# Two MLPs of a diffusion backbone: TensorE keeps the program's order instead of a planner's

## The chip, the cores and the metric

The kernel runs on one core of a Trainium2 chip. The time is device microseconds of one execution, and the median of the runs counts. TensorE (PE) multiplies matrices, VectorE (DVE) and ScalarE (ACT) work on vectors, GpSimd (POOL) does some of the vector work too, and SyncE (SP) issues the transfers. Each engine takes its own instructions strictly in the order in which they were written to its queue, and engines wait for one another by semaphores.

## The reference, cut to what matters

512 latent tokens and 256 context tokens, 1024 wide, pass two layers. Each layer is an attention sub-layer and then an MLP. Context tokens go through the MLP of layer 0 only, so that MLP has 768 tokens (6 tiles of 128) and the one of layer 1 has 512 (4 tiles).

```python
def sq_relu_mlp(h, w1, w2):          # w1: 1024 x 4096, w2: 4096 x 1024
    return jnp.square(jax.nn.relu(h @ w1)) @ w2

x = layer_norm(alpha * x + g_m * sq_relu_mlp(x * (1.0 + sc_m) + sh_m, mlp_w1[i], mlp_w2[i]),
               ln_g[i, 1], ln_b[i, 1])
```

The scales, shifts and gates (`sc_m`, `sh_m`, `g_m` and the like) come from a modulation map: a vector of 1024 numbers times `w_ada`, a 1024 x 6144 matrix per layer.

## The kernel before, in words

Every float32 operand is split into a high and a low part (`split_hi` on ACT, line 62; `split_lo` on DVE, line 65), and a product becomes three: high x high, high x low, low x high. For weights the parts are the tiles `wh` and `wl`, for hidden units `hh` and `hl`. A weight tile is loaded into one of 3 buffers `raw`, then split into one of 6 pairs of buffers `wh`/`wl`.

`mlp` (line 940) cuts the 4096 hidden units into 32 blocks of 128, taken as 16 groups of `G = 2`. For group c there are two kinds of work on PE:

- `up_mm(c)`, lines 977, 980 and 981: the first-matrix products, hidden = w1 x tokens, into the PSUM tag `big` (2 buffers). Layer 0: 96 products of 384 columns; layer 1: 48 of 512. `up_end(c)` then makes the hidden parts: relu on ACT (988), square on DVE (989), `hh` on ACT, `hl` on DVE. There are 4 buffers of each, two groups' worth.
- `down(i, hid, w2)`, lines 89 to 91 through `mm3`: the second-matrix products of token tile i, 12 products of 512 columns into two buffers of the PSUM tag `one` (4 buffers in all, so two tiles' worth). DVE adds each half to the accumulator `yacc` (line 1059; in group 0 ACT copies it, 1057).

In the program, layer 0 writes out group 0's first-matrix products ahead of the loop, layer 1 those of groups 0 and 1. The loop runs over c = 0 to 13: weights `w2(c)`, first-matrix products of c + 1 where they are not done, then `down` of group c for all tiles. At c = 13 each tile also gets `yacc * gate` (1061) and `+ alpha * x` (1062), where x is reloaded (`xr`, 2 buffers) and scaled by POOL (328, 329). The tail takes groups 14 and 15 together: four blocks, 24 products per token tile, then residual, LayerNorm and, in layer 1, the output.

In layer 0 the loop also carries the modulation vectors of later sub-layers as a filler: 56 steps, 5 per group, each loading a 512 KB slice of `w_ada` into `raw` and adding it, scaled, to `xr` accumulators (ACT 206, DVE 197, POOL 208). After 8 steps an `end` runs on PE: products with `onehot` (215), then, after a DVE addition (`modrow`, 132), for four of the seven vectors two transposes (152). `Fill` calls `end` after `lag` further calls; one call follows each token tile.

What sets the order: the order of each engine's queue is chosen at build time by a planner that simulates the program. Of the instructions that its simulation finds ready it takes the one that stands first in the program. So first- and second-matrix products of different groups may be mixed on PE. `tc.manual_schedule(engines=...)` takes an engine out of the planner's hands: its instructions keep program order. The planner also hands out the buffers of a tag.

Of the kernel before, what the change touches and what calls it, by code (L numbers as in the profile page):

```python
# [12 lines left out]
F32R = mybir.dt.float32r  # L13
# [6 lines left out]
P = 128  # L20
# [14 lines left out]
G = 2  # L35
R = 2
# [3 lines left out]
def backbone(ctx, tc, a, out):  # L40
# [3 lines left out]
    nc = tc.nc  # L44

    def pool(stack, name, bufs=1, side="left", space=None):
        kw = {"space": space} if space is not None else {"side": side}
        return stack.enter_context(tc.tile_pool(name=name, bufs=bufs, reuse_waits="tile", **kw))
# [6 lines left out]
    def big():  # L55
        return ps.tile([P, 2, 512], F32, name="big", tag="big", bufs=2)

    def one():
        return ps.tile([P, 512], F32, name="one", tag="one", bufs=4)

    def split_hi(dst, src):
        return nc.scalar.copy(out=dst, in_=src)  # L62
# [323 lines left out]
    accs = {t: pair[t // 2 - 1][:, t % 2, :] if t >= NCT else one() for t in range(NT)}  # L386
# [127 lines left out]
    fill = Fill(steps, 6)  # L514
# [425 lines left out]
    def mlp(layer, tiles, aH, aL, x_src, late, zst, lnst, fill, before_tail, finish):  # L940

        nt = len(tiles)
        ntok = nt * P
        n = NH // G
        st = ExitStack()
        hp = pool(st, "hp")
        ups = {}

        def up(c):
            if c not in ups:
                ws = [weight(a["mlp_w1"][layer, c * G + j]) for j in range(G)]
                if nt == 6:
                    Hs = [big()[:, :, 0:384] for j in range(G)]
                    parts = [[(H[:, i, :], i * 384, i * 384 + 384) for i in range(2)] for H in Hs]
                else:
                    H = big()
                    Hs = [H[:, j : j + 1, :] for j in range(G)]
                    parts = [[(h[:, 0, i * 256 : i * 256 + 256], i * 256, i * 256 + 256) for i in range(2)] for h in Hs]  # L960
                    if c > 1:
                        parts = [[(h[:, 0, :], 0, 512)] for h in Hs]
                ups[c] = (ws, Hs, parts)
            return ups[c]

        def up_mm(c, which=None, js=range(G), hooks={}):
            ws, Hs, parts = up(c)
            for j in js:
                wh, wl = ws[j]
                for i, (o, s, e) in enumerate(parts[j]):  # L970
                    if which is not None and i != which:
                        continue
                    for k in range(KD):
                        ks = slice(k * P, (k + 1) * P)
                        for f in hooks.get(k, []):
                            f()
                        mm = nc.tensor.matmul(o, wh[:, ks], aH[:, k, s:e], start=(k == 0), stop=False)  # L977
                        if k in hooks:
                            tc.keep_in_program_order(mm)
                        nc.tensor.matmul(o, wh[:, ks], aL[:, k, s:e], start=False, stop=False)  # L980
                        nc.tensor.matmul(o, wl[:, ks], aH[:, k, s:e], start=False, stop=(k == KD - 1))  # L981

        def up_end(c):
            out_h = []
            for Hv in up(c)[1]:
                r = hp.tile([P, ntok], F32, name="r", tag="r", bufs=2)
                rv = r.rearrange("p (c w) -> p c w", c=Hv.shape[1])
                nc.scalar.activation(rv, Hv, AF.Relu)
                nc.vector.tensor_tensor(out=r, in0=r, in1=r, op=ALU.mult)
                hh = hp.tile([P, ntok], F32R, name="hh", tag="hh", bufs=G * R)  # L990
                hl = hp.tile([P, ntok], F32R, name="hl", tag="hl", bufs=G * R)
                split_hi(hh, r)
                split_lo(hl, r, hh)
                out_h.append((hh, hl))
            return out_h

        def w2_of(c, gate=None):
            return [weight(a["mlp_w2"][layer, c * G + j], gate=gate) for j in range(G)]

        def down(i, hid, w2):  # L1000
            accs = [one(), one()]
            cols = slice(i * P, (i + 1) * P)
            m = len(hid)
            for hf in range(2):
                cs = slice(hf * 512, hf * 512 + 512)
                for j in range(m):
                    mm3(
                        accs[hf], hid[j][0][:, cols], hid[j][1][:, cols], w2[j][0][:, cs], w2[j][1][:, cs],
                        j == 0, j == m - 1,
                    )  # L1010
            return accs

        def temp():
            return hp.tile([P, ntok], F32, name="r", tag="r", bufs=2)[:, 0:512]

        first = range(1 if nt == 6 else 2)
        for c in first:
            up_mm(c, 0, range(G if c < first[-1] else G - 1))
        after, n_late = [], len(late)

        def act_step():
            after[:] = late.pop(0)()

        hooks = {}
        for k in range(n_late):
            hooks.setdefault(((5, 5, 7, 7) if layer == 0 else (2, 2, 7, 7))[k], []).append(act_step)
        up_mm(first[-1], 0, [G - 1], hooks)
        for c in first:
            up_mm(c, 1)
        hid = {c: up_end(c) for c in first}  # L1030
        zst.close()
        yp = pool(st, "yp")
        yacc = [yp.tile([P, D], F32, name=f"yacc{t}") for t in range(nt)]
        ln = LN(lnst, layer, 1, 2, 2)
        ln.gain(2 * layer)
        fill = Fill(fill(ln), 0)
        nfill = -(-len(fill.steps) // (n - R - 1))
        for c in range(n - R):
            with ExitStack() as order:
                for ins in after if c == 0 else []:  # L1040
                    order.enter_context(tc.issue_after(ins))
                w2 = w2_of(c)
                if c + 1 not in hid:
                    up(c + 1)
            if c + 1 not in hid:
                up_mm(c + 1)
                hid[c + 1] = up_end(c + 1)
            for i, t in enumerate(tiles):
                if c == n - R - 1:
                    x = ln.x_tile(x_src(t))  # L1050
                    g = ln.gate_tile(stream(t))
                    ln.affine(x, x)
                accs = down(i, hid[c], w2)
                for hf in range(2):
                    cs = slice(hf * 512, hf * 512 + 512)
                    if c == 0:
                        nc.scalar.copy(out=yacc[i][:, cs], in_=accs[hf])
                    else:
                        nc.vector.tensor_tensor(out=yacc[i][:, cs], in0=yacc[i][:, cs], in1=accs[hf], op=ALU.add)  # L1059
                if c == n - R - 1:  # L1060
                    nc.vector.tensor_tensor(out=yacc[i], in0=yacc[i], in1=g, op=ALU.mult)
                    nc.vector.scalar_tensor_tensor(
                        out=yacc[i], in0=x, scalar=ALPHA, in1=yacc[i], op0=ALU.mult, op1=ALU.add
                    )
                fill(i < nfill)

        one_gate = ln.gate_tile(stream(tiles[0])) if stream(tiles[0]) == stream(tiles[-1]) else None
        w2, hs = [], hid[n - R]
        for c in range(n - R + 1, n):
            w2 += w2_of(c - 1, one_gate)  # L1070
            up_mm(c)
            hs = hs + up_end(c)
        w2 += w2_of(n - 1, one_gate)
        fill.rest()
        ln.close_x()
        before_tail(ln, temp, yacc)
        for i, t in enumerate(tiles):
            accs = down(i, hs, w2)
            z = yacc[i]
            g = ln.gate_tile(stream(t))  # L1080
            for hf in range(2):
                cs = slice(hf * 512, hf * 512 + 512)
                if one_gate is not None:
                    nc.vector.tensor_tensor(out=z[:, cs], in0=z[:, cs], in1=accs[hf], op=ALU.add)
                    continue
                tmp = temp()
                nc.vector.tensor_tensor(out=tmp, in0=accs[hf], in1=g[:, cs], op=ALU.mult)
                eng = nc.gpsimd if i < nt - 1 else nc.vector
                eng.tensor_tensor(out=z[:, cs], in0=z[:, cs], in1=tmp, op=ALU.add)
            finish(ln, t, i, z)  # L1090
        st.close()
# [413 lines left out]
```

## Time and profile before

| | |
|---|---|
| median of 3 runs | 1697.6 us (1696.79 to 1701.78) |
| the profiled execution | 1703.23 us |
| its span | 1701.4 us |
| granted TensorE clock, mean | 0.989 |
| PE busy | 1629.9 us (96%) |
| DVE busy | 1111.5 us (65%) |
| ACT, POOL busy | 719.5 us (42%), 450.6 us (26%) |
| first product of the layer 0 MLP | at 412.5 us |
| first product of the layer 1 MLP | at 1316.9 us |

The span runs from the first to the last instruction; the execution's own time is 1.8 us longer. All stretches are in microseconds from the span's start. A timeline row gives start, duration, engine, line, operation, output <- inputs, shapes and count; a bracket tells how long the engine sat idle before it and which instruction ended the wait. Products are pipelined: a row's duration is longer than the distance to the next start, and what a product costs in a dense stretch is that distance.

### The profile page before, as it was taken

Reading aid. Unit: us, or ns where it says so; the run is one execution under the profiler, and the core shown is the slowest. Engines: PE = TensorE matmul, PEld = TensorE weight load, DVE = VectorE, ACT = ScalarE, POOL = GpSimd, SP = SyncE. Lnnn points to the kernel's source line nnn. Section 1 sums busy time; section 2 is a strip of 40 time slices with the busy share of each in tenths; the row PEclk is TensorE's granted clock in tenths of the full one; section 3 lists DMA queues with packets and bytes.
Section 4 is the critical chain, followed back from the end, with each engine's and each line's share of the span. In section 5 each row is a group of like instructions: output and inputs, shape, how many; then the busy total and the mean of one; then the engine's idle time right before and its main releaser. Section 6 shows DMA issues by size and latency. Waiting matters only on the chain.

```text
span 1701.4 us, 23714 instructions
## 1 busy us (share of the span) xinstructions
PE 1629.9 (96%) x9266; PEld 1369.1 (80%) x9266; DVE 1111.5 (65%) x1700; ACT 719.5 (42%) x1317; POOL 450.6 (26%) x317
## 2 busy tenths in 40 slices
PE   8997998999999999999999899999999999999996
PEld 6775776778888888898889798888778888888884
DVE  4778778755756666556447776766658655555577
ACT  3324666644633344333122356666663532222221
POOL 0247889000323345224003431000004200000034
PEclk9998999999999999999999999999999999999998
DMA  8312113033434356344212232001013533322322
GB/s 323 133 66 90 51 57 100 26 136 112 161 122 138 112 184 198 114 147 146 68 50 85 73 104 90 1 1 38 21 60 122 182 99 99 99 98 88 99 75 75
DMA packets 51969, 172.05 MB, mean 101 GB/s; under 512 B 6776, under 2 KB 6928, under 8 KB 51856
## 3 DMA queue, kind: packets, MB, share of 16 engines
q1 hardware_dynamic: 51824, 170.51, 29.8%
q8 instruction: 73, 1.20, 0.3%
q14 instruction: 40, 0.33, 0.1%
q10 hardware_dynamic: 32, 0.02, 0.0%
HBM read 161.03 MB, written 9.47 MB: 100 GB/s over the span
## 4 chain that ended last, share of the span: by engine, by line
PE 68%; DVE 12%; DMA 7%; POOL 6%; ACT 4%; issue 2%; SPq 0%; DVEq 0%; POOLq 0%; ACTq 0%
PE one L89 9%; PE one L91 9%; PE one L90 9%; PE big L977 7%; PE big L981 6%; PE big L980 6%; DMA araw<-in_w_ada_dram 4%; PE one L731 4%; PE one L917 2%; PE one L921 2%; PE one L918 2%; DVE wl L65 2%; PE one L707 2%; POOL aacc L208 2%; DMA raw<-in_mlp_w_dram 2%
## 5 line engine op out<-in xcount | busy, mean ns | idle before, releaser
L62 ACT CAST wh<-raw 128x1024 fp32r<-128x1024 f32 (+3 forms) x172 | 171.9, 1016 | 399.3 <-PE one L91 213.2
L65 DVE TENSOR_TENSOR wl<-raw,wh 128x1024 fp32r<-128x1024 f32 (+3 forms) x172 | 219.8, 1291 | 173.1 <-ACT wh L62 171.6
L977 PE MATMUL big<-actH,wh 128*128 128x384 f32 (+2 forms) x800 | 280.4, 351 | 1.6 <-ACT wh L62 1.6
L981 PE MATMUL big<-actH,wl 128*128 128x384 f32 (+2 forms) x800 | 279.7, 350 | 0.8 <-DVE wl L65 0.8
L980 PE MATMUL big<-actL,wh 128*128 128x384 f32 (+2 forms) x800 | 279.6, 350 | 0.0
L89 PE MATMUL one<-wh,hh 128*128 128x512 f32 x640 | 256.3, 402 | 12.6 <-ACT hh L62 7.0
L91 PE MATMUL one<-wh,hl 128*128 128x512 f32 x640 | 254.5, 399 | 5.3 <-DVE hl L65 5.3
L90 PE MATMUL one<-wl,hh 128*128 128x512 f32 x640 | 255.5, 399 | 1.3 <-DVE wl L65 1.3
L1059 DVE TENSOR_TENSOR yacc<-yacc,one 128x512 f32<-128x512 f32 x260 | 174.0, 682 | 109.9 <-PE one L91 109.6
L208 POOL TENSOR_TENSOR xr<-xr,raw 128x1024 f32<-128x1024 f32 x49 | 129.7, 2647 | 244.8 <-ACT raw L206 229.6
L977 PEld LDWEIGHTS big<-actH,wh 128*128 128x128 f32 x800 | 150.1, 188 | 15.0 <-ACT wh L62 2.4
L981 PEld LDWEIGHTS big<-actH,wl 128*128 128x128 f32 x800 | 150.1, 188 | 14.1 <-DVE wl L65 1.4
L980 PEld LDWEIGHTS big<-actL,wh 128*128 128x128 f32 x800 | 150.2, 188 | 12.3 <-issue 0.4
L89 PEld LDWEIGHTS one<-wh,hh 128*128 128x128 f32 x640 | 122.0, 191 | 44.5 <-ACT hh L62 8.0
L691 ACT ACTIVATE prob<-big,nm 128x768 f32<-128x768 f32 x128 | 116.2, 908 | 92.2 <-DVE nm L690 91.8
L91 PEld LDWEIGHTS one<-wh,hl 128*128 128x128 f32 x640 | 121.5, 190 | 35.0 <-DVE hl L65 6.2
L90 PEld LDWEIGHTS one<-wl,hh 128*128 128x128 f32 x640 | 122.1, 191 | 27.5 <-DVE wl L65 1.7
L328 POOL TENSOR_TENSOR xr<-xr,ln_g 128x1024 f32<-128x1024 f32 x14 | 37.2, 2658 | 390.9 <-DMA xr<-xres 384.6
L690 DVE TENSOR_REDUCE nm<-big 128x1 f32<-128x768 f32 x128 | 119.8, 954 | 31.8 <-PE big L1360 19.0
L707 PE MATMUL one<-ident,prob 128*128 128x128 f32 x832 | 104.8, 275 | 2.9 <-ACT pT L710 2.0
L731 PE MATMUL one<-pT,V 128*64 128x256 f32 x768 | 98.0, 391 | 5.7 <-DVE pT L712 4.5
L707 PEld LDWEIGHTS one<-ident,prob 128*128 128x128 f32 x832 | 96.0, 142 | 6.8 <-ACT pT L710 2.7
(245 smaller groups left out, 2822.9 us busy)
## 6 DMA issues: line engine op xcount, KB each, us to landing
raw<-in_mlp_w_dram SPq DMA_DIRECT2D x128, 512.0 KB
raw<-in_w_ada_dram SPq DMA_DIRECT2D x56, 512.0 KB
sraw<-in_w_ada_dram SPq DMA_DIRECT2D x16, 512.0 KB
araw<-in_w_ada_dram SPq DMA_DIRECT2D x32, 256.0 KB
raw<-in_w_o_dram SPq DMA_DIRECT2D x16, 512.0 KB
xr<-xres SPq DMA_DIRECT2D x14, 512.0 KB
raw<-in_w_qkv_dram SPq DMA_DIRECT2D x12, 512.0 KB
xres<-z SPq DMA_DIRECT2D x10, 512.0 KB
```

The costliest lines, as they stand in the source:

```text
L62: return nc.scalar.copy(out=dst, in_=src)
L65: return nc.vector.tensor_tensor(out=dst, in0=src, in1=hi.bitcast(F32), op=ALU.subtract)
L89: nc.tensor.matmul(o, lh, rh, start=start, stop=False)
L90: nc.tensor.matmul(o, lh, rl, start=False, stop=False)
L91: nc.tensor.matmul(o, ll, rh, start=False, stop=stop)
L208: nc.gpsimd.tensor_tensor(out=accs[s], in0=accs[s], in1=dst, op=ALU.add)
L707: nc.tensor.transpose(tp[:, j * P : (j + 1) * P], pts[j % 2][:, k * P : (k + 1) * P], ident)
L731: nc.tensor.matmul(acc[64 * hh : 64 * hh + 64, 0:256], v(kts[n], hh), PT[:, :, n, hh, :], start=(n == 0), stop=(n == len(kts) - 1),)
L977: mm = nc.tensor.matmul(o, wh[:, ks], aH[:, k, s:e], start=(k == 0), stop=False)
L980: nc.tensor.matmul(o, wh[:, ks], aL[:, k, s:e], start=False, stop=False)
L981: nc.tensor.matmul(o, wl[:, ks], aH[:, k, s:e], start=False, stop=(k == KD - 1))
L1059: nc.vector.tensor_tensor(out=yacc[i][:, cs], in0=yacc[i][:, cs], in1=accs[hf], op=ALU.add)
```

## The change

PE's queue in the loop and in the first part of the tail of both MLPs is pinned to program order. In layer 1 the program is moved so that first-matrix products run two groups ahead (`ahead = 2`) with three groups' worth of `hh`/`hl` buffers; layer 0 stays one ahead. `Fill`'s lag goes from 0 to 2. In the tail, the first two token tiles are begun with three of the four blocks, both of them, before the fourth block follows for both; after that the pin ends.

```diff
+        ahead = 1 if nt == 6 else 2
...
-                hh = hp.tile([P, ntok], F32R, name="hh", tag="hh", bufs=G * R)
-                hl = hp.tile([P, ntok], F32R, name="hl", tag="hl", bufs=G * R)
+                hh = hp.tile([P, ntok], F32R, name="hh", tag="hh", bufs=G * (ahead + 1))
+                hl = hp.tile([P, ntok], F32R, name="hl", tag="hl", bufs=G * (ahead + 1))
...
-        def down(i, hid, w2):
-            accs = [one(), one()]
+        def down(i, hid, w2, accs=None, js=None):
+            accs = accs or [one(), one()]
...
-                for j in range(m):
+                for j in range(m) if js is None else js:
...
-        fill = Fill(fill(ln), 0)
+        fill = Fill(fill(ln), 2)
         nfill = -(-len(fill.steps) // (n - R - 1))
+
+        pinned = ExitStack()
+        pinned.enter_context(tc.manual_schedule(engines={nc.tensor.engine}))
         for c in range(n - R):
             with ExitStack() as order:
                 for ins in after if c == 0 else []:
                     order.enter_context(tc.issue_after(ins))
                 w2 = w2_of(c)
-                if c + 1 not in hid:
-                    up(c + 1)
-            if c + 1 not in hid:
-                up_mm(c + 1)
-                hid[c + 1] = up_end(c + 1)
+                for d in range(c + 1, c + ahead + 1):
+                    if d not in hid:
+                        up(d)
+            for d in range(c + 1, c + ahead + 1):
+                if d not in hid:
+                    up_mm(d)
+                    hid[d] = up_end(d)
...
         for c in range(n - R + 1, n):
             w2 += w2_of(c - 1, one_gate)
-            up_mm(c)
-            hs = hs + up_end(c)
+            if c not in hid:
+                up_mm(c)
+                hid[c] = up_end(c)
+            hs = hs + hid[c]
         w2 += w2_of(n - 1, one_gate)
         fill.rest()
         ln.close_x()
         before_tail(ln, temp, yacc)
+        m = len(hs)
+        begun = {i: down(i, hs, w2, None, range(m - 1)) for i in range(2)}
+        for i in range(2):
+            down(i, hs, w2, begun[i], [m - 1])
+        pinned.close()
         for i, t in enumerate(tiles):
-            accs = down(i, hs, w2)
+            accs = begun[i] if i in begun else down(i, hs, w2)
```

## Rows read from the trace of the kernel before

**Rows 1.** Stretches: length, busy PE, PEld, DVE, ACT, POOL (instructions), granted clock, DMA.
```profile
449.00:640.00 191.00, 182.37 (x927) 159.45 (x926) 120.44 (x123) 78.93 (x86) 64.16 (x24) 1.00 0.44 143
640.00:905.00 265.00, 264.83 (x1341) 237.00 (x1340) 148.28 (x170) 84.12 (x88) 67.38 (x27) 1.00 0.36 121
905.00:960.00 55.00, 50.18 (x228) 43.01 (x228) 45.85 (x39) 10.10 (x12) 25.34 (x10) 0.94 0.25 82
1343.00:1352.00 9.00, 6.22 (x19) 4.72 (x20) 8.92 (x8) 4.56 (x7) 4.15 (x2) 0.81 0.30 104
1352.00:1660.00 308.00, 308.00 (x1324) 248.35 (x1324) 176.12 (x218) 89.39 (x116) 18.62 (x7) 1.00 0.29 94
1660.00:1690.00 30.00, 25.90 (x100) 20.09 (x98) 23.74 (x33) 4.54 (x7) 11.98 (x8) 0.89 0.13 45
```

**Rows 2.** Timeline of ACT and PE in layer 1's steady state.
```profile
1517.08 2.00 ACT L62 CAST wh<-raw 128x1024 fp32r<-128x1024 f32 x2 [8.26 <-PE one L91]
1520.81 1.05 ACT L62 CAST wh<-raw 128x1024 fp32r<-128x1024 f32 x1 [1.73 <-PE big L980]
1526.41 1.05 ACT L62 CAST wh<-raw 128x1024 fp32r<-128x1024 f32 x1 [4.55 <-PE big L980]
...
1526.21 0.40 PE L981 MATMUL big<-actH,wl 128*128 128x512 f32 x1
1526.44 0.39 PE L89 MATMUL one<-wh,hh 128*128 128x512 f32 x1
```

**Rows 3.** Timeline of PE where layer 1's first second-matrix products begin.
```profile
1342.93 0.50 PE L89 MATMUL one<-wh,hh 128*128 128x512 f32 x1 [1.09 <-ACT hh L62]
...
1347.83 0.79 PE L91 MATMUL one<-wh,hl 128*128 128x512 f32 x1 [2.78 <-DVE hl L65]
...
1350.98 0.52 PE L89 MATMUL one<-wh,hh 128*128 128x512 f32 x1
```

**Rows 4.** Timeline of DVE, POOL and PE at layer 1's tail.
```profile
1649.32 1.21 DVE L1061 TENSOR_TENSOR yacc<-yacc,gate 128x1024 f32<-128x1024 f32 x1
1661.99 3.27 POOL L329 TENSOR_TENSOR xr<-xr,ln_b 128x1024 f32<-128x1024 f32 x1
1662.91 3.42 DVE L1061 TENSOR_TENSOR yacc<-yacc,gate 128x1024 f32<-128x1024 f32 x1
...
1669.92 0.79 PE L89 MATMUL one<-wh,hh 128*128 128x512 f32 x1 [3.61 <-ACT hh L62]
...
1675.20 0.54 PE L89 MATMUL one<-wh,hh 128*128 128x512 f32 x1
```

**Rows 5.** Timeline of PE at layer 0's tail.
```profile
943.19 0.50 PE L89 MATMUL one<-wh,hh 128*128 128x512 f32 x1 [2.25 <-ACT hh L62]
...
946.50 0.79 PE L91 MATMUL one<-wh,hl 128*128 128x512 f32 x1 [2.57 <-DVE hl L65]
...
952.07 0.39 PE L89 MATMUL one<-wh,hh 128*128 128x512 f32 x1
```

**Rows 6.** Timeline in layer 0's loop: a wait for a PSUM buffer, two filler ends.
```profile
530.48 0.50 PE L89 MATMUL one<-wh,hh 128*128 128x512 f32 x1 [2.81 <-DVE yacc L1059]
...
564.70 1.09 PE L215 MATMUL one<-xr,onehot 128*32 128x256 f32 x16
565.72 0.50 PE L89 MATMUL one<-wh,hh 128*128 128x512 f32 x1
565.92 0.42 DVE L132 TENSOR_TENSOR modrow<-one,brow 128x256 f32<-128x256 f32 x1 [0.42 <-PE one L215]
570.03 0.38 PE L152 MATMUL one<-ident,modrow 128*128 128x128 f32 x2
...
601.52 2.40 POOL L208 TENSOR_TENSOR xr<-xr,raw 128x1024 f32<-128x1024 f32 x1 [2.46 <-ACT raw L206]
611.97 0.50 PE L89 MATMUL one<-wh,hh 128*128 128x512 f32 x1
614.07 0.41 DVE L132 TENSOR_TENSOR modrow<-one,brow 128x256 f32<-128x256 f32 x1
```

## The prediction, made before the changed kernel was run

> **What bounds the kernel now.** I read the page's shares first: PE is busy nearly all of the span, so the question is where inside the two MLPs it is not. The table of stretches answers that [rows 1]. In layer 1 from 1352 to 1660 us PE is busy 308.00 of 308.00 us with 1324 recorded products, 0.233 us each, at the full clock; in layer 0 from 640 to 905 us it is busy 264.83 of 265.00. No order can be faster there. What can be won lies at four places: the first part of layer 0's loop (191.00 - 182.37 = 8.6 us idle), layer 0's tail, and layer 1's beginning and tail, where the granted clock also falls below 1 (0.94, 0.81, 0.89).
>
> Next comes the timeline at those places. At layer 1's beginning PE waits 1.09 us for `hh` and 2.78 us for `hl` of the hidden groups that were finished last; then 7 starts take 3.15 us (1347.83 to 1350.98), 1.5 us more than at 0.233 [rows 3]. At layer 1's tail it waits 3.61 us for `hh`, and 12 starts take 5.28 us, 2.5 too many [rows 4]. At layer 0's tail it waits 2.25 and 2.57 us, and 13 starts take 5.57 us, 2.5 too many [rows 5]. The slow starts are 0.43 us apart, the lower of the clock's two levels (1.2 instead of 2.4 GHz), right behind a wait of about 3 us. So these three places hold 5.4, 6.1 and 7.3 us. In layer 0's loop a typical wait is for DVE to empty a PSUM buffer, the longest one 2.81 us [rows 6]. All four together: 27.4 us, 1.6% of the time. That is the ceiling.
>
> **The change part by part.** The sum is made against the profiled execution, 1703.2 us (span 1701.4); the median of the runs, 1697.6, lies 5.6 below it, and I carry the difference over to it.
>
> *Steady state.* No product is added or removed. In layer 1 the planner already runs two groups ahead: at 1526.44 second-matrix products start 0.23 us after the last first-matrix product, too soon to use what that one made, so they use an earlier group [rows 2]. The pin writes down nearly the same order, only unmixed. What it could break is the supply of weights. Six pairs of buffers hold three groups' halves; a new split waits for a used one. The trace shows pairs of splits released by the end of second-matrix work (line 91, 1517.08) and pairs released by first-matrix work (line 980, 1520.81 and 1526.41), always as soon as a pair is free [rows 2]. So a freed buffer goes to the next weight in the program. In the new order the first-matrix products of group c + 2 finish before `down` of c starts, their buffers take the first-matrix weights of c + 3, and those are split 11.2 us (48 x 0.233) before they are needed. Cost 0; DVE has 176.12 of 308 us of work there [rows 1]. The transfers of w1 move one group forward on SP, in the order in which the planner had them already.
>
> *Layer 1's beginning.* The first-matrix products of group 2, 48 x 0.233 = 11.2 us, now stand before `down` of group 0. The hidden parts that PE waits for end at 1347.8 [rows 3], and PE would ask for them about 1353 instead of 1341.7. The waits go, and with them the low clock. What is late next is `wl` of group 2's first block, which the third of these products needs; its buffer comes free while group 1's products still run. Between 0 and -5.4; I take -5.4.
>
> *Layer 1's tail.* Group 15's first-matrix products move in front of `down` of group 13, so its hidden parts have 48 more products' time, 11.2 us, plus the first six of the tail. The wait was 3.61 us. It goes, the low clock too: -6.1. Against it: at group 13 DVE has per tile two additions, line 1061 and line 1062, and in the old order PE's 11.2 us of group 15 came behind that work and gave DVE time. Bound on the other side: two of the contended steps of 3.42 us [rows 4] delay the emptying of PSUM by 6.8, of which the spare pair of PSUM buffers hides one token tile (12 x 0.233 = 2.8): +4. I take -6.1, because the emptying reads PSUM and comes first in the program.
>
> The Trainium skill (SBUF — State Buffer, Who interferes with whom) speaks against this: a DVE step with two SBUF inputs and a GpSimd step that reads SBUF exclude each other for a whole instruction. The trace agrees: line 1061 takes 1.21 us alone and 3.42 us beside POOL's line 329 [rows 4]. By that rule every such step of the tail that meets POOL would take the long time, and the tail would win nothing; that is the first rival.
>
> *Layer 0's tail.* Here the order stays one ahead, so group 15 is still made last. New is that tiles 0 and 1 do three blocks each before the fourth: its block is needed 36 products, 8.4 us, into the tail instead of 9 products. The third block is still needed after 6 products, 1.4 us, as before, and DVE is as backed up as before (45.85 busy of 55 us, [rows 1]). Between 0 and -7.3; I take the middle, -3.6.
>
> *The filler in layer 0's loop.* Four of the seven ends have transposes. On PE the planner had put other products between line 215 and line 152: 565.72 to 570.03 [rows 6]. Pinned, the transposes stand right behind line 215 and wait for DVE's `modrow`; behind them on PE wait the next token tile's 12 products, behind these DVE's additions, which have nothing else to do for it. Price from two rows: 565.92 + 0.42 - 565.72 = 0.6 us where DVE was free, 614.07 + 0.41 - 611.97 = 2.5 us where it was not [rows 6]. I take 1.5: 4 x 1.5 = +6 (bounds +2.4 and +10). The lag of 2 instead of 0 puts an end one call, one token tile, later. That is cover for its accumulators: the tightest was done at 603.9 and read at 610.9 [rows 6], 7 us earlier. The two accumulators come free 2.8 us later, the next vector's transfers and steps (SP, ACT, DVE, POOL) with them; POOL is busy 64.16 of 191 us there [rows 1] and takes that up.
>
> *Emptying PSUM in layer 0's loop.* The old order mixed first-matrix products between token tiles, the new one runs six tiles in one stretch, 72 x 0.233 = 16.8 us. DVE must empty 12 halves in it, and its filler steps stand in between. Fewer pauses for DVE within a stretch, but none of this work in the 16.9 us of the first-matrix stretch. Between -8.6 (all waits go) and +22 (second rival); nearest is the row itself, so I take 0.
>
> Sum: -5.4 - 6.1 - 3.6 + 6 + 0 = -9.1. Profiled execution 1694.1, median **1688.5**, told as 1688.
>
> **The rivals.** *Backlog (no change).* DVE and POOL share out the last groups' work as they do now, and both tails win nothing: -5.4 + 6 = +0.6, so 1698. For it: DVE is busy 23.74 of 30 and 45.85 of 55 us at the tails [rows 1]. Against it: in layer 1 the hidden parts are now due 11 us later than made.
>
> *Emptying falls behind (slower).* Place: `down` of groups 1 to 11 in layer 0, while the filler runs. PE's order no longer holds first-matrix products that are ready while DVE is late, so every late emptying stops PE. Price: one wait of 2.81 us [rows 6] in each of 11 groups is 31 us in place of 8.6: +22.3. With the sum above +13.2, so 1711. It decides from the point where DVE's work inside one stretch exceeds 16.8 us plus the spare token tile's 2.8. For it: DVE is at 120.44 of 191 us [rows 1], and half of its work could fall into the stretch beside the 12 additions. Against it: DVE's filler steps go by when slices land, which is spread evenly.
>
> *Buffers by a fixed rotation (slower).* If weights took the six buffers in turn, first-matrix weights of the next group would wait for `down` before them in every group: a split of 1.05 and a low part of 1.2 us, less two products, 1.8 us x 26 groups = 47, so 1736. The alternating releases speak against it [rows 2].
>
> *All waits go (faster still).* -27.4 with the low transposes' price, +2.4: -25, so 1673; half of the loop's and layer 0's tail's waits gives 1679. For it: PE's queue then never depends on a simulated time that the chip doesn't keep. Against it: DVE and POOL slow each other whatever PE does.
>
> **How the numbers follow.** A measurement of this kernel tells about 0.3%, 5 us, from no change. Forecast 0.54 (its own range 1682 to 1695), backlog 0.18, emptying 0.10, rotation 0.03, all waits 0.15. Faster than 1692.5: 0.15 and 0.49 of the forecast's 0.54: 0.64. Within: 0.05 of the forecast and 0.16 of backlog: 0.21. Slower: the rest of backlog 0.02 and the two slower rivals: 0.15. The range 1677 to 1702 leaves out most of the slower rivals (0.13) and the lower end of the last (0.07).
>
> **What would show it.** Right: in layer 1 no PE wait for `hh` or `hl`, first-matrix stretches of 48 unbroken, the granted clock 1.00 from 1343 to the end of the products; four waits of line 152 for `modrow` of 0.6 to 2.5 us. Wrong: waits of line 89 for `yacc` (line 1059) in most layer 0 groups (emptying), waits of line 977 or 981 for `wh` or `wl` in every group (rotation), or PE waits of 3 us at either tail (backlog).

## The result, and the profile after

The changed kernel takes 1722.1 us (median of 4 runs, 1719.7 to 1728.1); the kernel before, run beside it on the same chip, 1697.8. The ratio is 1.0141, with a 95% interval from 1.0118 to 1.0163: slower, where 1688 had been forecast, with a range that ended at 1702.

The profiled execution took 1728.1 us (span 1726.3), 24.9 us more than the one of before. I cut both traces at the same products on PE. The part ahead of the layer 0 MLP, in which no code differs, is 1.8 us longer by chance (over all runs below it took 406.7 to 414.2 us). Layer 0's loop, from its first to its last first-matrix product, went from 526.9 to 554.0 us: +27.1. From there to layer 1's first MLP product: 377.5 and 377.0, -0.6. From there to the end: 384.5 and 381.1, -3.4. These add up to 24.9.

The stretches of after that answer to [rows 1], moved by what had been lost until then (columns as there):

```profile
451.00:668.00 217.00, 199.80 (x975) 173.07 (x974) 135.57 (x136) 86.35 (x93) 72.45 (x28) 0.96 0.42 139
668.00:933.00 265.00, 257.29 (x1289) 228.91 (x1288) 142.34 (x157) 76.64 (x81) 57.46 (x23) 0.99 0.33 110
933.00:988.00 55.00, 50.23 (x229) 43.24 (x229) 49.21 (x40) 10.09 (x12) 26.20 (x10) 0.94 0.26 82
1371.00:1386.00 15.00, 13.01 (x49) 9.78 (x48) 13.00 (x12) 7.23 (x10) 3.86 (x2) 0.89 0.36 120
1386.00:1690.00 304.00, 304.00 (x1306) 244.76 (x1305) 169.90 (x217) 89.44 (x117) 10.37 (x5) 1.00 0.28 91
1690.00:1718.00 28.00, 20.25 (x86) 15.69 (x84) 23.07 (x36) 2.35 (x3) 22.99 (x13) 0.99 0.22 78
```

The fifth row is as forecast: PE is busy 304.00 of 304.00 us. The first two are not: 17.2 us idle instead of 8.6, 7.7 instead of 0.2, and the granted clock below 1. Who ended PE's waits in layer 0's loop (us in total, times, longest), first in the kernel before:

```profile
PE one L89 <- DVE yacc L1059: 3.0, 2, 2.8
PE one L89 <- ACT yacc L1057: 2.1, 1, 2.1
PE big L977 <- ACT wh L62: 1.6, 2, 1.1
PE one L90 <- DVE wl L65: 1.3, 1, 1.3
PE big L981 <- DVE wl L65: 0.8, 2, 0.6
```

and in the changed kernel:

```profile
PE one L89 <- DVE yacc L1065: 9.4, 6, 2.1
PE big L978 <- ACT wh L62: 7.4, 1, 7.4
PE one L152 <- DVE modrow L132: 5.6, 4, 3.9
PE one L89 <- ACT yacc L1063: 2.1, 1, 2.1
PE big L982 <- DVE wl L65: 0.3, 1, 0.3
```

That is 24.8 us of waits against 8.8: +16. Products with no wait in front of them that start more than 0.08 us later than the dense distance (0.176 us behind a product of 384 columns, 0.233 behind one of 512) lose 12.2 us against 3.1, summed over the loop: +9. I call these late starts. About 9 of the 12.2 us fall into five stretches, 23.9 us long in all, in which the granted clock was 0.50; in the loop of the kernel before it was 1.00 throughout, so its 3.1 us, and about 3 of the 12.2, are not the clock's. Of the other 2 us less than one lies at the filler ends' products; the rest is in smaller delays. So PE waits for three things: DVE's additions, one weight, and the transposes' input.

One of the additions' waits, in the changed kernel's timeline:

```profile
523.88 3.42 DVE L197 SCALAR_TENSOR_TENSOR xr<-raw,scT,xr 128x1024 f32<-128x1024 f32 x1
527.38 1.15 ACT L206 ACTIVATE raw<-raw,scT 128x1024 f32<-128x1024 f32 x1 [5.27 <-DVE xr L197]
528.43 1.04 ACT L62 CAST wh<-raw 128x1024 fp32r<-128x1024 f32 x1
528.67 2.41 POOL L208 TENSOR_TENSOR xr<-xr,raw 128x1024 f32<-128x1024 f32 x1 [2.46 <-ACT raw L206]
529.51 2.65 DVE L65 TENSOR_TENSOR wl<-raw,wh 128x1024 fp32r<-128x1024 f32 x1 [2.21 <-ACT wh L62]
532.09 0.68 DVE L1065 TENSOR_TENSOR yacc<-yacc,one 128x512 f32<-128x512 f32 x1
532.82 0.74 PE L89 MATMUL one<-wh,hh 128*128 128x512 f32 x1 [2.05 <-DVE yacc L1065]
```

`down` of this group began at 525.02, so the first half to be emptied was complete at 526.6. DVE did not touch it until 532.09, yet it was not simply overworked: it sat idle for 2.21 us, because the next instruction of its queue was the low split of a weight whose cast ACT had not made; the split then took 2.65 us beside POOL's addition, where it takes 1.22 alone; the addition stood behind it. ACT's cast in turn stood behind a filler step that waited 5.27 us for DVE. The Trainium skill (PSUM — Partial Sum Buffer, Engine vs sequencer instructions) says that the queues of ScalarE, VectorE and GpSimd are strict FIFO; the rows of ACT and DVE agree.

This wait has a twin in the kernel before, the 2.81 us at 530.48 [rows 6], in front of which DVE idled 1.34 us for a cast and then took 2.65 us for the split; so the chain is old, and the length of this wait is no part of the loss (the lower clock behind it is). Four others are new: 1.56 us at 495.38, 2.14 at 617.14, 1.36 at 689.91 and 1.81 at 731.04. In front of them DVE idled 5.74, 2.68, 3.69 and 1.75 us for a cast of ACT; behind the last two of these pauses the split also took 3.18 and 2.60 us beside POOL. The longest of the four, where no split was lengthened and the weight itself came late:

```profile
613.31 1.05 ACT L62 CAST wh<-raw 128x1024 fp32r<-128x1024 f32 x1 [3.53 <-DMA raw<-in_mlp_w_dram]
614.39 1.22 DVE L65 TENSOR_TENSOR wl<-raw,wh 128x1024 fp32r<-128x1024 f32 x1 [2.68 <-ACT wh L62]
616.40 0.68 DVE L1065 TENSOR_TENSOR yacc<-yacc,one 128x512 f32<-128x512 f32 x1
617.14 0.50 PE L89 MATMUL one<-wh,hh 128*128 128x512 f32 x1 [2.14 <-DVE yacc L1065]
```

The weight wait, the largest:

```profile
571.88 1.09 PE L215 MATMUL one<-xr,onehot 128*32 128x256 f32 x16
573.05 2.19 ACT L206 ACTIVATE xr<-raw,scT 128x1024 f32<-128x1024 f32 x2 [6.78 <-PE one L215]
576.84 8.52 POOL L208 TENSOR_TENSOR xr<-xr,raw 128x1024 f32<-128x1024 f32 x3 [31.47 <-PE one L91]
579.63 7.16 SPq L69 DMA_DIRECT2D raw<-in_mlp_w_dram  x4
583.08 1.04 ACT L62 CAST wh<-raw 128x1024 fp32r<-128x1024 f32 x1 [1.15 <-DMA raw<-in_mlp_w_dram]
588.70 1.04 ACT L62 CAST wh<-raw 128x1024 fp32r<-128x1024 f32 x1 [1.22 <-DMA raw<-in_mlp_w_dram]
589.79 0.69 PE L978 MATMUL big<-actH,wh 128*128 128x384 f32 x1 [7.38 <-ACT wh L62]
```

Until the filler's end has read the accumulators (571.88), the next vector's loads, already landed, hold all three `raw` buffers; then POOL's additions free them one after the other, and only at 579.63 does SP issue weights: two of the second matrix first, then those of the first matrix, the third of which is cast at 588.70. PE wanted it at 582.4. In the kernel before the same filler end stood at 564.70 [rows 6]. From there to the third cast it took as long, 17.0 us against 16.8, but the planner had 72 second-matrix products behind the end and ahead of these first-matrix ones, where the fixed order with its later end had 36; so there the cast was in time:

```profile
581.73 1.05 ACT L62 CAST wh<-raw 128x1024 fp32r<-128x1024 f32 x1 [1.36 <-DMA raw<-in_mlp_w_dram]
...
584.39 0.33 PE L977 MATMUL big<-actH,wh 128*128 128x384 f32 x1
```

And the longest wait of the transposes, whose `modrow` stood in DVE's queue behind a late and lengthened split and two halves:

```profile
756.81 3.23 DVE L65 TENSOR_TENSOR wl<-raw,wh 128x1024 fp32r<-128x1024 f32 x1 [3.65 <-ACT wh L62]
757.98 0.64 PE L215 MATMUL one<-xr,onehot 128*32 128x256 f32 x8
759.97 0.67 DVE L1065 TENSOR_TENSOR yacc<-yacc,one 128x512 f32<-128x512 f32 x1
...
762.03 0.41 DVE L132 TENSOR_TENSOR modrow<-one,brow 128x256 f32<-128x256 f32 x1
762.50 0.69 PE L152 MATMUL one<-ident,modrow 128*128 128x128 f32 x2 [3.88 <-DVE modrow L132]
```

Last, layer 0's tail, layer 1's beginning and layer 1's tail, which answer to [rows 5], [rows 3] and [rows 4]:

```profile
960.53 0.81 ACT L989 ACTIVATE r<-big 128x768 f32<-128x768 f32 x1
969.53 3.09 DVE L990 TENSOR_TENSOR r<-r 128x768 f32<-128x768 f32 x1
973.54 0.80 PE L89 MATMUL one<-wh,hh 128*128 128x512 f32 x1 [3.82 <-ACT hh L62]
...
1377.14 0.50 PE L978 MATMUL big<-actH,wh 128*128 128x512 f32 x1 [1.45 <-ACT wh L62]
1378.40 0.50 PE L982 MATMUL big<-actH,wl 128*128 128x512 f32 x1 [0.54 <-DVE wl L65]
...
1694.88 2.39 POOL L329 TENSOR_TENSOR xr<-xr,ln_b 128x1024 f32<-128x1024 f32 x1
1697.31 3.38 DVE L1068 SCALAR_TENSOR_TENSOR yacc<-xr,yacc 128x1024 f32<-128x1024 f32 x1 [4.76 <-POOL xr L329]
1701.34 0.50 PE L89 MATMUL one<-wh,hh 128*128 128x512 f32 x1 [2.56 <-DVE yacc L1097]
```

### The profile page after: what moved, and what is told of

It is laid out like the page before. It is cut to its first block, busy times and chain, and to the rows that moved or that the text cites. A ratio compares the mean times of both kernels' runs of the same rounds, so it can differ in the third digit from the quotient of the medians.

```text
span 1726.3 us, 23698 instructions
## 1 busy us (share of the span) xinstructions
PE 1638.6 (95%) x9266; PEld 1373.5 (80%) x9266; DVE 1120.1 (65%) x1700; ACT 719.3 (42%) x1317; POOL 448.1 (26%) x317
## 4 chain that ended last, share of the span: by engine, by line
PE 67%; DVE 15%; DMA 6%; ACT 5%; POOL 3%; issue 3%; DVEq 0%; SPq 0%; ACTq 0%; POOLq 0%
PE one L89 9%; PE one L91 8%; PE one L90 8%; PE big L978 6%; PE big L982 5%; PE big L981 5%; PE one L731 5%; DMA raw<-in_w_ada_dram 4%; DVE wl L65 3%; PE one L707 2%; PE one L917 2%; POOL xr L208 2%; PE one L921 2%; PE one L918 2%; DVE nm L690 2%
## 5 line engine op out<-in xcount | busy, mean ns | idle before, releaser
L65 DVE TENSOR_TENSOR wl<-raw,wh 128x1024 fp32r<-128x1024 f32 (+3 forms) x172 | 234.9, 1379 | 229.8 <-ACT wh L62 228.4
L978 PEld LDWEIGHTS big<-actH,wh 128*128 128x128 f32 x800 | 151.0, 189 | 20.5 <-ACT wh L62 9.7
```

The lines of the kernel that those rows point to most:

```text
L65: return nc.vector.tensor_tensor(out=dst, in0=src, in1=hi.bitcast(F32), op=ALU.subtract)
```

## The experiments

"Loop" below is layer 0's loop in the profiled execution, which took up to 6.4 us more or less than its kernel's median; the ratios to the kernel before, each against runs on the same chip, decide. "Waits" and "late starts" are counted as above; what the lower clock costs is a part of the late starts. Theory S (supply): weights come late, and the engines' queues stand behind them. Theory E (emptying): DVE has too much work to empty PSUM in time, as the second rival of the prediction had it.

| run | loop | waits | late starts | ratio (95%) |
|---|---|---|---|---|
| before | 526.9 | 8.8 | 3.1 | 1 |
| changed | 554.0 | 24.8 | 12.2 | 1.0141 (1.0118 to 1.0163) |
| layer 1 only | 528.1 | 7.6 | 5.5 | 0.9976 (0.9963 to 0.9989) |
| lag 0 | 547.5 | 22.5 | 7.9 | 1.0101 (1.0082 to 1.0119) |
| first-matrix weights first | 554.5 | 24.7 | 12.7 | 1.0097 (1.0071 to 1.0122) |
| spread | 551.7 | 23.9 | 11.6 | 1.0084 (1.0062 to 1.0107) |
| no additions | 534.5 | 13.0 | 5.8 | 1.0012 (0.9997 to 1.0027) |
| additions not from raw | 546.3 | 20.5 | 9.5 | 1.0085 (1.0065 to 1.0105) |
| filler on DVE | 532.3 | 11.8 | 4.2 | 1.0010 (1.0001 to 1.0020) |
| before, no additions | 519.5 | 2.5 | 3.2 | 0.9947 (0.9930 to 0.9965) |
| layer 1 only, filler on DVE | 516.5 | 0.4 | 2.0 | 0.9925 (0.9910 to 0.9941) |
| before, filler on DVE | 516.4 | 0.4 | 2.0 | 0.9936 (0.9921 to 0.9952) |
| filler on DVE, lag 0 | 530.6 | 9.1 | 5.2 | 1.0004 (0.9993 to 1.0016) |
| the same, ends cut | 532.0 | 9.4 | 6.5 | 1.0000 (0.9988 to 1.0012) |
| the same, first weights first | 519.9 | 1.6 | 3.0 | 0.9946 (0.9930 to 0.9962) |
| filler on DVE, first weights first | 530.7 | 10.0 | 4.2 | 1.0005 (0.9994 to 1.0017) |
| lag 0, first weights first | 543.5 | 18.9 | 8.0 | 1.0076 (1.0059 to 1.0093) |

**Layer 1 only.** Layer 0 as before.

```diff
-        pinned.enter_context(tc.manual_schedule(engines={nc.tensor.engine}))
+        if nt == 4:
+            pinned.enter_context(tc.manual_schedule(engines={nc.tensor.engine}))
...
-        fill = Fill(fill(ln), 2)
+        fill = Fill(fill(ln), 0 if nt == 6 else 2)
...
-        begun = {i: down(i, hs, w2, None, range(m - 1)) for i in range(2)}
+        begun = {i: down(i, hs, w2, None, range(m - 1)) for i in range(2 if nt == 4 else 0)}
```

> Layer 0's MLP as in the kernel before (order left to the planner, filler ends without lag, tail unchanged), layer 1's as in the changed kernel. Theory A (the loss of 24 us lies in layer 0's loop alone; layer 1's order pays): layer 0 from its first MLP product to the last first-matrix product back to 527 us, layer 1 shorter by 3.3 us as between the two traces: 1694, 0.2% faster than before. Rival B (the order costs in both layers and layer 1 only looks better because layer 0 left it other conditions): 1698 or more, with PE waits over 3 us at layer 1's beginning or tail.

0.24% faster, and the loop is back at 528.1. Theory A holds: layer 1's part of the change pays (379.2 us from its first MLP product to the end, against 384.5 before), layer 0's loses some 1.6%.

**Lag 0.** `Fill(fill(ln), 0)` in the changed kernel.

> The changed kernel with the filler's lag put back from 2 to 0, so that each filler end stands on PE two token tiles (5.6 us) earlier. Theory S (supply: the first 8 us wait, of products of group 5 for their weights, comes from the filler's end at 571.88, which frees the accumulators and with them the raw buffers and SP's queue): that wait falls from 7.5 to about 2 us and the low clock behind it (2.5 us) goes: 1714. Theory E (emptying of PSUM by DVE is most of the loss): no change, 1722. Rival L (without the lag the ends catch DVE and POOL too early, the accumulators are not done): PE waits at line 215 for xr, several us each, 1722 to 1735.

The gain of 0.4% (with intervals that touch) is what theory S said, if not by its steps: the weight wait fell from 7.4 to 4.9 us only, the late starts by 4.3. The expectation had the size of the step wrong: with lag 0 an end stands one token tile earlier, not two. 240 second-matrix products stand ahead of the second end instead of 252, 12 products or 2.8 us, and the wait fell by 2.5. No wait for accumulators came. The lag holds about a quarter of the loss.

**First-matrix weights first.**

```diff
-                w2 = w2_of(c)
                 for d in range(c + 1, c + ahead + 1):
                     if d not in hid:
                         up(d)
+                w2 = w2_of(c)
```

> The changed kernel, but in each group the weights of the next first-matrix products are loaded ahead of the second-matrix weights, which is the order in which TensorE now uses them. Theory S: in the changed kernel the four weights behind the filler were cast at 583.08, 586.43, 588.70 and 590.68, and the first-matrix products need the third: with it as the first they start 5.6 us earlier and the low clock behind the wait goes (2.5 us): 1714. The six waits of 1.5 to 2.3 us in second-matrix stretches stay. Theory E: only those waits count, 1722.

The waits for that weight and its low part fell from 7.6 to 3.5 us, 4.1 where 5.6 was expected, and the median by the 0.4% expected, though the two intervals overlap. The profiled execution shows no gain: its other waits rose by as much, to 14.5 us for additions from 11.5 and to 6.8 at the transposes from 5.6.

**Spread.**

```diff
             for i, t in enumerate(tiles):
+                if nt == 6 and i < 4:
+                    up_mm(c + 1, i % 2, [i // 2])
+                    if i == 3:
+                        hid[c + 1] = up_end(c + 1)
                 accs = down(i, hid[c], w2)
```

(and the products of c + 1 no longer stand ahead of the tiles in layer 0.)

> The changed kernel, but in layer 0's loop the 96 first-matrix products of group c + 1 are written in four parts of 24 between the token tiles of group c (part, tile, part, tile, part, tile, part, tile, tile, tile), still a fixed order. Theory E (DVE cannot empty two halves in each 2.8 us while it also has the filler's steps): the waits in second-matrix stretches, 18.6 us in the changed kernel, fall to the 10 us of the kernel before or less, and the waits of the filler's transposes shrink; the wait at layer 0's tail is not touched: 1711 to 1714. Theory S: the weights behind the filler are needed 17 us earlier in the group than before, that wait grows or stays: 1722 or more.

0.57% better than the changed kernel, about the time that theory E gave, but its mechanism fails: with twice the time for four of the six token tiles, the waits for additions are 14.5 us. What fell is the weight wait (to 4.6 us) and the transposes' (to 4.8). At 729.19 DVE began a low split after 7.90 us of idling for the cast, and the additions stood behind it. A fixed order with the products spread out is no remedy.

**No additions by POOL**, in the changed kernel and in the one before.

```diff
-                if k > 0:
+                if k > 0 and pools[1] is not None:
                     nc.gpsimd.tensor_tensor(out=accs[s], in0=accs[s], in1=dst, op=ALU.add)
```

> The changed kernel with the filler's POOL additions left out (all but the first product of a stream that went through POOL are lost, so the modulation vectors differ); DVE's filler steps, all transfers, ACT's products, the filler ends with their transposes and the fixed order stay. What goes is POOL's 2.4 to 3.0 us per step, which holds the filler's raw buffer. Theory S (supply: weights come late because the filler's steps hold the three raw buffers until POOL has added; ACT's and DVE's queues stand still behind the late cast): the 7.5 us weight wait and nearly all waits for DVE's additions go, layer 0's loop falls from 554 to 520 to 527 us: ratio to the kernel before 0.993 to 0.998. Theory E (DVE has too much work in a second-matrix stretch): DVE's work is the same but for what POOL lengthens it: 1.007 or more.

> The kernel before with the filler's POOL additions left out in the same way (the same part of the modulation is lost). It is the floor that the run without additions of the changed kernel is compared with. Theory S: the planner's order and the fixed order come to the same loop time when the raw buffers come free early, within 5 us (517 to 522 here, 520 to 527 there), layer 1 aside: ratio 0.993 to 0.997. Rival P (the fixed order costs by itself, through transposes behind the vector ends and stretches of 72 products): the loop here stays 12 us or more below the one there.

The first is 1.3% faster than the changed kernel; its waits for additions are 0.4 us, down from 11.5, with DVE's steps unchanged in number. So the additions were late because of POOL. DVE still idles 135.9 us in front of weight splits for a cast, more than the 108.5 of the changed kernel: the sum of such pauses says nothing, only whether additions are due behind one. But a weight wait of 5.9 us and 6.5 us at the transposes stayed, and the loop is 15 us longer than in the kernel before without additions: there theory S missed and rival P was right. The fixed order has a price of its own.

**Additions that hold no raw buffer.** POOL does the same number of additions of the same size.

```diff
+                    add = accs[s] if pools[1] is None else dst
-                    nc.gpsimd.tensor_tensor(out=accs[s], in0=accs[s], in1=dst, op=ALU.add)
+                    nc.gpsimd.tensor_tensor(out=accs[s], in0=accs[s], in1=add, op=ALU.add)
```

> The changed kernel, but the filler's POOL additions add the accumulator to itself in place of ACT's product (so the modulation vectors differ): POOL does the same 49 additions of two 128x1024 inputs beside DVE, but no longer holds the raw buffers. Theory H (the hold of the raw buffers makes weights late): as with no additions at all, ratio 0.999 to 1.004, loop 531 to 540 us. Theory C (contention: DVE's steps beside POOL take 2.6 to 3.4 us in place of 1.2, and that makes DVE late): as the changed kernel, ratio 1.011 to 1.016, loop 548 us or more. In between: both have a part, in proportion.

In between: 0.56 of the 1.3% came back, and 0.73 needs the additions themselves gone. What the hold does shows at SP: from 449 to 820 us its loads into `raw` waited 150.5 us in 41 places for POOL's additions in the changed kernel, and here not once for POOL but 103.4 us for ACT's products. But the two causes are not cleanly parted, since POOL's additions, which read one tile now, also lengthened DVE's steps less: the low splits took 1441 ns on average, against 1576 in the changed kernel and 1291 without additions. Both theories have a part; how large each is stays open.

**The filler on DVE**: its multiply-adds run on DVE, none on ACT and POOL.

```diff
-        mult = lambda k, s: "dve" if s == 0 and k > 0 else "act"
+        mult = lambda k, s: "dve"
...
-                1, v, 0, 1, (0, 1) if v < 2 else (0,), pools, mult if v < 2 else lambda k, s: "act"
+                1, v, 0, 1, (0, 1) if v < 2 else (0,), pools, mult
```

> The changed kernel with all multiply-adds of the filler on DVE (1.28 us each, frees the raw buffer itself) and none on ACT and POOL (1.15 + 2.4 to 3.0 us). DVE gets more work, the supply of raw buffers gets shorter: the two theories have opposite signs. Theory S: waits in layer 0's loop fall, above all behind 570 us: loop 530 to 540 us, ratio 1.000 to 1.006. Theory E: five more steps of 1.28 us per group of 33.8 us on DVE, more waits for its additions: ratio 1.014 to 1.022.

> Layer 0 as in the kernel before, layer 1 as in the changed kernel, and all multiply-adds of the filler on DVE. Theory S: the waits of layer 0's loop that are left (9 us, weights and additions) halve: ratio 0.994, faster than with layer 1's order alone (0.998). Theory E: DVE's added work shows as waits for its additions: ratio 1.000 to 1.006.

> The kernel before, with the filler's multiply-adds on DVE and nothing else changed. Theory S: the planner's order holds other work ready when weights are late, so it gains less from the better supply than the fixed order did (1.3%): its waits in layer 0's loop were 13 us with the low clock, so at most 0.7%; ratio 0.993 to 0.997, and the run with layer 1's order as well (0.9925) stays ahead of it by 0.1 to 0.3%.

All three went as theory S says; theory E has the wrong sign. DVE's costliest groups in the loop (busy, mean ns, idle before), first in the changed kernel:

```profile
L65 DVE TENSOR_TENSOR wl<-raw,wh 128x1024 fp32r<-128x1024 f32 x62 | 97.0, 1576 | 108.5 <-ACT wh L62 108.5
L65 DVE TENSOR_TENSOR hl<-r,hh 128x768 fp32r<-128x768 f32 x30 | 40.2, 1340 | 15.2 <-ACT hh L62 15.2
```

and with the filler on DVE:

```profile
L197 DVE SCALAR_TENSOR_TENSOR xr<-raw,scT,xr 128x1024 f32<-128x1024 f32 x70 | 87.9, 1281 | 34.5 <-DMA raw<-in_w_ada_dram 33.6 <-ACT xr L206 0.7
L65 DVE TENSOR_TENSOR wl<-raw,wh 128x1024 fp32r<-128x1024 f32 x62 | 78.9, 1286 | 70.3 <-ACT wh L62 70.1
L65 DVE TENSOR_TENSOR hl<-r,hh 128x768 fp32r<-128x768 f32 x30 | 28.6, 953 | 5.4 <-ACT hh L62 5.4
```

So DVE's steps are shorter, and a filler step frees its raw buffer when it ends. PE's waits that were left:

```profile
PE big L978 <- ACT wh L62: 6.1, 1, 6.1
PE one L152 <- DVE modrow L132: 3.0, 4, 1.3
PE one L89 <- DVE yacc L1065: 2.5, 4, 0.8
PE big L982 <- DVE wl L65: 0.2, 1, 0.2
```

With the planner's order in layer 0 the same edit leaves 0.4 us of waits in all; with layer 1's order added it is the fastest kernel here, 0.9925. By the ratios it is open whether layer 1's order still adds to it, since 0.9925 and 0.9936 have overlapping intervals; in the two traces the part from layer 1's first MLP product to the end takes 379.1 us with it and 384.5 without.

**What the fixed order still costs.** Lag 0, then the filler end cut in two, so that the transposes stand one token tile later on PE:

```diff
-            ada_finish(layer, v, half, n, o, bias[0])
+            if n > 1:
+                return ada_finish(layer, v, half, n, o, bias[0])
+            row = ada_row(o[:, 0:q], bias[0])
+            return lambda: ada_finish(layer, v, half, n, o, None, row)
...
-                self.ends.pop(0)[1]()
+                more = self.ends.pop(0)[1]()
+                if more is not None:
+                    self.ends.insert(0, (self.n + 1, more))
```

and then the first-matrix weights first as well.

> The changed kernel with the filler's multiply-adds on DVE (as in the run before) and the lag put back from 2 to 0. Theory S': the one weight wait of 6 us that was left with the filler on DVE (at 572) comes from the lag alone: with it an end stands two token tiles later, and the next vector's loads hold all three raw buffers until that end has freed the accumulators. It falls under 1 us, the low clock behind it goes too: loop 532 to 524 us or less, ratio 0.996 to 0.997. Rival: the wait moves to another place (ends too early for DVE, PE waiting at line 215), ratio 1.000 or more.

> The run before this one, with the filler end cut in two: the two transposes stand one token tile (12 products) later on PE than the products that make their input. Theory P1 (what the fixed order still costs is the transposes' wait for DVE): their four waits of 0.6 to 1.3 us, and the low clock behind them, go; loop 2 to 4 us shorter than without the cut, ratio 0.994 to 0.995, and layer 0's loop then comes to within 4 us of the 516 us that the planner's order reaches with the filler on DVE. Rival: the end's PSUM buffer, held one token tile longer, leaves one buffer less for the additions: no gain, new waits for DVE's additions.

> The same, with the first-matrix weights loaded ahead of the second-matrix weights of a group. If the supply still decides, another 1 to 3 us; if it no longer does (the theory), no change against the run with the cut: ratio within 0.001 of it, apart from about 1 us at layer 1's beginning, where its second block's low part was late.

I was wrong on all three. Lag 0 left 3.2 of the 6.1 us of the weight wait, again about one token tile less. With the cut the transposes' waits went to zero, but a weight wait of 4.0 and 5.1 us for additions stood in their place: no gain, as the rival said, though that the held PSUM buffer is the reason was not shown. Only the third step, for which the theory expected nothing, brought 0.54%: the weight waits went, and one line is left:

```profile
PE one L89 <- DVE yacc L1070: 1.6, 4, 0.8
```

So the order of the loads counts. Does it alone?

> The changed kernel with two edits: the filler's multiply-adds on DVE, and the first-matrix weights of a group loaded ahead of its second-matrix weights. Lag 2 and the uncut filler ends stay. Theory S (order of supply decides: the first products of the fixed order are the first-matrix ones, their weights came second): the 6 us weight wait at 572 of the run with the filler on DVE alone goes, loop 532 to 522 to 524 us, ratio 0.995 to 0.997. Rival (the lag or the uncut ends matter as much): a weight wait over 2 us stays, ratio 0.999 to 1.001 as with the filler on DVE alone or with lag 0.

> The changed kernel with the first-matrix weights loaded first and lag 0, the filler's products and additions left on ACT and POOL. Theory S: each of the two edits alone gave 0.4% of the 1.4%; together the weight wait is gone, but POOL's additions still hold the raw buffers and DVE's queue still stands behind late casts: waits for DVE's additions of 8 to 12 us stay, ratio 1.005 to 1.008. Rival (order of loads and lag are the whole cause, POOL's hold only adds to it): ratio 0.998 to 1.002.

No: with lag 2 and uncut ends 2.7 us of weight waits, 3.0 at the transposes and 4.3 for additions stay, and nothing is gained. With lag 0 but POOL's additions kept, 14.5 us of waits for additions stay (theory S, which said 8 to 12). Each edit by itself moves a wait to the next late thing; together the four (filler on DVE, lag 0, ends cut, first weights first) take the fixed order to within 4 us of the planner's loop with the filler on DVE (519.9 and 516.4 us). Whether the cut is needed for that was not tried.

## Why the prediction was wrong

For the profiled execution the forecast was 34.0 us too low (1694.1 against 1728.1): 1.8 us the unchanged part ahead, 11.1 us of gains that did not come, 21.1 us of loss in layer 0's loop that was not in the sum (+27.1 against the +6 of the transposes).

*Steady state (0): right.* In layer 1 not one PE wait for `hh` or `hl`, unbroken stretches of 48, full clock; weights in time.

*Layer 1's beginning (-5.4).* The waits for `hh` and `hl` went, as said. I had named the low part of group 2's first block as late next; both parts of its second block were: 1.45 + 0.54 us, and eight starts 0.43 us apart behind, at the lower clock. The loss there fell from 5.9 us (3.9 of waits, 2.1 of late starts) to 4.1 (2.0 and 2.1) only: right step, size too large.

*Layer 1's tail (-6.1).* The wait for `hh` went. In its place PE waits 2.56 us for an addition, which stands in DVE's queue behind line 1068, idle for 4.76 us until POOL has made the normalised input; POOL had itself waited 16.70 us for the load of it (line 328 at 1689.70). The bound on the other side, DVE and POOL delaying the emptying, came true in part. The Trainium skill (SBUF — State Buffer, Who interferes with whom) says that a DVE instruction with two SBUF inputs contends with a GpSimd instruction that reads SBUF; the trace agrees here too (3.38 us for line 1068 beside POOL, 1.22 at 1685.00, where POOL was idle). Both places of layer 1: -11.5 forecast; measured were -4.9 to the last product and +1.6 in the output behind it, -3.4 in all. With layer 0 left as before it was -5.3, so the chance in such a figure is about 2 us.

*Layer 0's tail (-3.6).* -0.6, and the waits there are 4.8 us in both kernels. ACT had made the third block's relu at 961.3; DVE squared it at 969.53, behind its backlog. The backlog rival was right for this place.

*Transposes (+6).* 5.6 us of waits: 0.60, 0.60, 3.88 and 0.55. Three at the price of the lower bound and one beyond that of the upper: that the sum is right is luck, and the low clock behind the longest is not in it.

*Supply of weights and emptying of PSUM in layer 0's loop (0): the steps that failed.* I argued the weights' supply on layer 1's rows, where no filler runs, and carried the 0 over to layer 0. There the filler shares the three raw buffers and SP's queue with the weights, and the change moved two things against each other: the filler's end later (lag 2), the first-matrix products earlier, with their weights still loaded second. I had also put the lag at nothing, because POOL "takes that up"; taking the lag back won 0.4%. For the emptying I had the right rival, *emptying falls behind*, and the reason that fixed products no longer fill a wait; with or without additions, with the filler on POOL or DVE, the fixed order as it was changed costs 15 us or more against the planner's. But I tied its threshold to DVE's amount of work, and found it unlikely. DVE was busy 337 of 554 us; what counts is what stands first in its queue, and how long POOL stretches that.

*Low clock.* I counted it at three places, 1.5 and twice 2.5 us, and left it out of the loop, where waits were priced at their length. There 9 us were lost in products at the granted clock of 0.50, at all five waits of 2 us or more. The two such waits of the kernel before (2.06 and 2.81 us) had none; the same two waits with layer 1's order alone, 2.08 and 2.71 us, had it. So a part of this loss changes from execution to execution.

*Rivals.* No fixed rotation: one long wait of line 978, not one in each group. The emptying's place and sign were right, its price of +22 was not: I had called the wait of 2.81 us typical, but it was the only long one of its kind in that loop, and the changed kernel has six such waits with 9.4 us in all, not 11 of 2.81. The loss is made of them, of one weight wait and of the transposes, in part with the low clock behind.

What stays open: how the waits of the two causes, held buffers and lengthened DVE steps, divide at each place, since the one run that was to separate them also lets POOL's additions run earlier and lengthen DVE's steps less.

## What to carry to other kernels

A fixed order of one engine is only as good as the order in which its inputs arrive: when the order is turned round, look at the order of the loads too, and follow every buffer that they share with other work; here turning the loads round paid clearly only once the other late things had been mended. An idle engine can be the late one: look at what stands at the head of its in-order queue, not at its busy share. And a wait on TensorE can cost more than its length: the 24.8 us of waits here came with 9 us lost at the lower clock.

## What was not expected of the hardware

Taking 49 multiply-adds of 1.28 us onto DVE (63 us) raised DVE's busy time in the loop by 12 us only (337 to 349): with POOL silent the weights' low splits went from 1576 to 1286 ns on average, the hidden ones from 1340 to 953 and the filler's own steps from 1833 to 1281. Work given to POOL was paid for twice, on POOL and in DVE's steps beside it.
